# A two-block transformer kernel: five Q column blocks and half of the K splits become filler of the band attention, the bias table leaves by ScalarE's queue, and the rotary embedding runs on VectorE alone

## The chip, the cores and the metric

The kernel runs on one core of one Trainium2 chip. The core has TensorE (PE in the rows; PEld is its weight load), VectorE (DVE), ScalarE (ACT), GpSimd (POOL) and SyncE (SP), which here only issues DMAs. The metric is the device time of one execution in microseconds.

## The reference, cut to what matters

The program is two residual blocks, one after the other, on 512 tokens of width 1024. The change touches only the first block, which runs its layer twice (`DEPTH = 2`):

```
z = rms_norm(x, g) @ w_in[l]
q, k, v, cb, cc, cx, ga, gb = split(z)        # q 16 heads x 64, k and v 4 x 64, the rest 1024 each
q = partial_rope(q);  k = partial_rope(k)     # the first 16 of 64 dims are rotated
y_attn = band_attention(q, k, v, sink) @ w_attn_proj      # window of +-128 tokens
y_conv = (cb * short_conv(cc * cx, conv_w)) @ w_conv_proj # 3 taps along the tokens
mix = (sigmoid(ga) * y_attn + sigmoid(gb) * y_conv) @ w_out
x = x + rms_norm(mix);  x = x + rms_norm(ffn(rms_norm(x)))
```

The second block has four other attentions. Two of them add a bias that is looked up by distance in a small table (32 buckets by 8 heads). The kernel computes that table while the first block still runs, because the first block does not need it.

## The kernel before

Everything is feature-major: 128 features by 512 tokens are one block, and a matrix of 1024 features is eight blocks. The weights are packed on the host into units of 128x1024 float32 (512 KB), in the order in which they are used. A `Stream` loads a unit on SP's queue into one of three `raw` buffers (L255), ScalarE casts it to its high part `wh` (L267), and VectorE subtracts to get the low part `wl` (L268). One block of a product (`mblock`) is 24 matmuls: for each of 8 input blocks high x high, low x high and high x low (L513, L514, L515). A unit is cut two units ahead of its use, and a layer cuts 3 (layer 0) or 4 (layer 1) units beyond V ahead of time (`CA`).

After the norm, a layer does the following. The head computes K (two blocks, `pk`) and the first Q block; then V. VectorE forms the cosine and sine tables times the norm's factor (`ropeR`, L555). `rope` rotates a block: a multiplication of the PSUM block by the cosines (L563) and a shuffle of it (L564), both on VectorE, then a multiplication by the sines (L565) and a sum (L566), both on GpSimd. Each K head is split into `KH` (two casts on ScalarE, L577 and L578) and `KL` (two subtractions on VectorE, L579 and L580). Each Q block is split the same way (L595, L596). Before, all four K heads are split, V is evacuated (L586, L587), and all eight Q blocks are computed, rotated and split before the attention starts.

The band attention walks 16 heads in 18 steps: scores S, transposes of the softmax one step later, the product with V two steps later. Between these pieces it calls filler work from a list `bg`: before, the 24 blocks of the convolution branch (`conv_cc`, `conv_cx`, `conv_cb` for each of 8 columns). The order in which instructions stand on each engine is set by a scheduler of the framework, and each engine runs its list strictly in order.

The framework also gives each DMA one of eight completion semaphores in turn (DMAHW0 to DMAHW7). A DMA waits for the earlier DMA that used the same semaphore, whichever queue issued it.

After layer 0's attention, `bias_tables` makes the eight bias rows of 640 values with two small products, copies them to `row` (8 partitions), and writes each row 128 times to DRAM (`bias_d`, 2.62 MB) for the second block (L859). Then come eight blocks with the gate `gb` (L634) and eight with `w_conv_proj` (L639).

Of the kernel before, what the change touches and what calls it, by code (L numbers as in the profile page):

```python
# [9 lines left out]
F32 = mybir.dt.float32  # L10
F32R = mybir.dt.float32r
# [3 lines left out]
P = 128  # L15
T = 512
D = 1024
NB = 8
DEPTH = 2
NH = 16  # L20
# [8 lines left out]
U = 1024  # L29
# [35 lines left out]
def fm_units(w):  # L65
    m = w.shape[1] // P
    return w.reshape(NB, P, m, P).transpose(2, 1, 0, 3).reshape(m, P, U)


def tm_units(w, per):  # L70
    c = w.shape[1]
    u = w.reshape(NB // per, per, P, c).transpose(0, 2, 1, 3).reshape(NB // per, P, per * c)
    if per * c < U:
        u = np.concatenate([u, np.zeros((u.shape[0], P, U - per * c), u.dtype)], axis=2)
    return u


def down_units(w):
    t = w.reshape(NF, P, NB, P).transpose(2, 0, 1, 3).reshape(NF, 8, P, P)
    return t.transpose(0, 2, 1, 3).reshape(NF, P, U)  # L80


def pack(inp):
    units = []

    def put(u):
        units.append(u)

    for l in range(DEPTH):
        w = inp["w_in"][l]  # L90
        put(fm_units(w[:, 1024:1280]))
        put(fm_units(w[:, 0:128]))
        put(tm_units(w[:, 1280:1536], 4))
        put(fm_units(w[:, 128:1024]))
        cc, cx, cb = (fm_units(w[:, o:o + 1024]) for o in (2560, 3584, 1536))
        put(np.stack([cc, cx, cb], axis=1).reshape(24, P, U))
        put(fm_units(w[:, 5632:6656]))
        put(fm_units(inp["w_conv_proj"][l]))
        put(np.stack([fm_units(w[:, 4608:5632]), fm_units(inp["w_attn_proj"][l])], axis=1).reshape(16, P, U))
        put(fm_units(inp["w_out"][l]))  # L100
        put(np.stack([fm_units(inp["w_gate"][l]), fm_units(inp["w_up"][l])], axis=1).reshape(2 * NF, P, U))
        put(down_units(inp["w_down"][l]))
    w = inp["w_in_2"][0]
    o = np.cumsum([0, 256, 256, 256, 256, 256, 256, 4, 256, 256, 256, 256, 64, 64, 64, 64, 64, 64, 12])
# [7 lines left out]
    g = cat(dvs, dvw, bf, dg, dks, dkw)  # L112
    g = np.concatenate([g.reshape(NB, P, 272), np.zeros((1, P, 272), g.dtype)]).reshape(3, 3, P, 272)
    g = g.transpose(0, 2, 1, 3).reshape(3, P, 816)
# [70 lines left out]
    rope = np.stack([np.tile(ct, (2, 1)), np.tile(st, (2, 1))], axis=1).reshape(P, 2 * T)  # L185
# [94 lines left out]
class Kern:  # L280
# [249 lines left out]
    def layer(self, l, tail, pend):  # L530
        nc = self.nc
        h = Pair(self, "h", NB)
        acc2 = self.tmp("acc2")
        rs = {}
        head = Head(self, h, 3, seq=l == 0)
# [4 lines left out]
        pk = head.ps[0:2]  # L540
        wv = [self.st.next(ahead=1 + i) for i in range(2)]
        pv = [self.ps("pv") for _ in range(2)]
        for kb in range(NB):
            w = wv[kb // 4]
            sl = slice((kb % 4) * 256, (kb % 4) * 256 + 256)
            for tb in range(4):
                o = pv[tb // 2][:, (tb % 2) * 256:(tb % 2) * 256 + 256]
# [10 lines left out]
        C, S = cs[:, 0, :], cs[:, 1, :]  # L558
        perm = [(i + 8) % 16 if i < 16 else i for i in range(32)]

        def rope(ps):
            t1, t2 = self.tmp("t1"), self.tmp("t2")
            nc.vector.tensor_mul(t1, ps, C)  # L563
            nc.vector.stream_shuffle(t2, ps, perm)  # L564
            nc.gpsimd.tensor_mul(t2, t2, S)  # L565
            nc.gpsimd.tensor_add(t1, t1, t2)  # L566
            return t1

        KH, KL = FM(self, "KH", NKV, F32R), FM(self, "KL", NKV, F32R)
        lo_h, hi_h = slice(0, 64), slice(64, 128)  # L570
        for m in range(2):
            k = rope(pk[m])
            for j in range(2):
                src = k[64 * j:64 * j + 64]
                g = 2 * m + j
                own, oth = (lo_h, hi_h) if j == 0 else (hi_h, lo_h)
                nc.scalar.copy(KH[g][own], src)  # L577
                nc.scalar.copy(KH[g][oth], src)  # L578
                nc.vector.tensor_sub(KL[g][own], src, KH[g][own].bitcast(F32))  # L579
                nc.vector.tensor_sub(KL[g][oth], src, KH[g][own].bitcast(F32))  # L580
        V = FM(self, "V", 4, F32R)
        for tb in range(4):
            src = pv[tb // 2][:, (tb % 2) * 256:(tb % 2) * 256 + 256].rearrange("p (g d) -> p g d", g=4)
# [2 lines left out]
            nc.scalar.activation(vv[:, :, 0, :], src, AF.Copy, scale=r)  # L586
            nc.vector.scalar_tensor_tensor(vv[:, :, 1, :], src, r, vv[:, :, 0, :].bitcast(F32),  # L587
                                           op0=OP.mult, op1=OP.subtract)
        Q = FM(self, "Q", NH, F32R)
        for m in range(NB):  # L590
            q = rope(head.ps[2] if m == 0 else self.mblock(h))
            for j in range(2):
                hd = 2 * m + j
                own, oth = (lo_h, hi_h) if j == 0 else (hi_h, lo_h)
                nc.scalar.copy(Q[hd][own], q[own])  # L595
                nc.vector.tensor_sub(Q[hd][oth], q[own], Q[hd][own].bitcast(F32))  # L596

        y = FM(self, "y", NB, F32)
        cw = f"conv_w{l}"
# [20 lines left out]
            nc.vector.tensor_mul(t, self.mblock(h), self.R)  # L620
            nc.gpsimd.tensor_mul(y[m], t, cur.pop("c"))

        bg = [lambda m=m, f=f: f(m) for m in range(NB) for f in (conv_cc, conv_cx, conv_cb)]
        o = FM(self, "o", NB, F32)
        self.attend = True
        self.band_attention(l, Q, KH, KL, V, o, bg)
        self.attend = False
# [14 lines left out]
        for m in range(NB):  # L642
            g = self.tmp("ga")
# [100 lines left out]

    def band_attention(self, l, Q, KH, KL, V, o, bg):
        nc = self.nc
# [11 lines left out]
        def S(h):  # L758
# [4 lines left out]
            for i in range(4):  # L763
                n = HI[i] - LO[i]
                ps = self.ps("s")
                q = Q[h][:, i * P:(i + 1) * P]
                nc.tensor.matmul(ps[:, :n], q, KH[g][:, LO[i]:HI[i]], start=True, stop=False)  # L767
# [74 lines left out]
    def bias_tables(self):  # L842
        nc = self.nc
        oh = self.blk("oh", [33, 768], F32)
        nc.sync.dma_start(oh, self.a["onehot"])
        tab = self.small("tab", [33, 8], bufs=1)
        nc.sync.dma_start(tab, self.a["tab"])
        ohr = self.blk("ohr", [33, 768], F32R)
        nc.vector.tensor_copy(ohr, oh)
        tabr = [self.small(n, [33, 8], F32R, bufs=1) for n in ("tabh", "tabl")]  # L850
        self.split(*tabr, tab)
        row = self.blk("row", [8, 640], F32)
        for c0, c1, c2 in ((0, 512, 512), (512, 768, 640)):
            ps = self.ps("tb")
            for i, t in enumerate(tabr):
                nc.tensor.matmul(ps[0:8, :c1 - c0], t, ohr[:, c0:c1], start=i == 0, stop=i == 1)
            nc.scalar.copy(row[:, c0:c2], ps[0:8, :c2 - c0])
        self.bias_d = self.dramp.tile([8, P, 640], F32, name="bias_d")
        nc.sync.dma_start(self.bias_d, row[:, None, :].to_broadcast([8, P, 640]))  # L859

    def load_bias(self, h0):
        F = FM(self, "F", 4, F32)
# [530 lines left out]

    def sb_head(self, hd, Q, KH, KL, V, o):
        nc = self.nc
# [327 lines left out]
```

## Time and profile before

| | |
|---|---|
| time, median of 3 runs | 2560.83 us (2558.83 to 2562.65) |
| span of the profiled execution | 2559.2 us |
| TensorE busy | 2430.2 us, 95% of the span |
| VectorE busy | 1401.1 us, 55% |
| ScalarE busy | 1009.1 us, 39% |
| GpSimd busy | 500.3 us, 20% |
| mean granted TensorE clock | 0.973 of full speed |

The times are of whole executions; the span is that of the one execution that was profiled, from its first to its last instruction. TensorE is nearly always busy, so the table says where to look: at the few stretches in which TensorE is idle, or runs at a lower granted clock.

### The profile page before, as it was taken

The page shows a single profiled execution, that of the slowest core. Times are in us where ns is not written, and L with a number is a line of the kernel's source. Part 1 is how long each engine was busy: PE and PEld are TensorE (multiplying, and loading weights), DVE is VectorE, ACT ScalarE, POOL GpSimd, SP SyncE. Part 2 cuts the span into 40 slices and gives each one's busy share as a digit, 9 for nine tenths or more (in the row PEclk, how much of TensorE's full clock was granted, in tenths as well). Part 3 has the DMA queues.
Part 4 walks back from the last instruction along what each step waited for, and adds up shares of the span by engine and source line. Part 5 has one row for each costly group of instructions (what it writes and reads, how often), then busy time and mean ns, then how long its engine had stood idle before and what let it go on. Part 6 is the DMA issues. An engine that isn't in the chain of part 4 may idle for free.

```text
span 2559.2 us, 32881 instructions
## 1 busy us (share of the span) xinstructions
PE 2430.2 (95%) x12680; PEld 2090.4 (82%) x12680; DVE 1401.1 (55%) x2426; ACT 1009.1 (39%) x1885; POOL 500.3 (20%) x549
## 2 busy tenths in 40 slices
PE   8999779989999988999999899999698899999999
PEld 7888668888888887888888888888697888988888
DVE  7777343366643268776533676422667787644431
ACT  5455232343223243554323432222366576333320
POOL 4323000141110045321001411100411232100000
PEclk9999989989999999999999899999899899999999
DMA  4222442245423231213323354232320214222250
GB/s 140 85 73 71 86 121 91 82 141 196 180 102 124 91 128 42 75 66 103 107 82 99 124 214 180 92 98 91 106 88 26 82 44 132 80 93 93 95 179 29
DMA packets 84860, 264.37 MB, mean 103 GB/s; under 512 B 9023, under 2 KB 17855, under 8 KB 84704
## 3 DMA queue, kind: packets, MB, share of 16 engines
q1 hardware_dynamic: 84704, 262.27, 30.7%
q8 instruction: 100, 1.64, 0.3%
q14 instruction: 56, 0.46, 0.1%
HBM read 247.03 MB, written 15.20 MB: 102 GB/s over the span
## 4 chain that ended last, share of the span: by engine, by line
PE 87%; DVE 7%; ACT 2%; another core or an unknown queue 2%; issue 1%; POOL 0%; DMA 0%; SPq 0%; DVEq 0%; POOLq 0%; ACTq 0%
PE ps L513 24%; PE ps L515 24%; PE ps L514 23%; PE o L817 1%; PE pt L792 1%; PE tm L998 1%; PE tm L999 1%; PE tm L1000 1%; PE hd L514 1%; PE hd L513 1%; PE hd L515 1%; DVE wl L268 1%; PE s L768 1%; PE s L767 1%
## 5 line engine op out<-in xcount | busy, mean ns | idle before, releaser
L268 DVE TENSOR_TENSOR wl<-raw,wh 128x1024 fp32r<-128x1024 f32 x382 | 474.8, 1260 | 378.1 <-ACT wh L267 318.2
L267 ACT CAST wh<-raw 128x1024 fp32r<-128x1024 f32 x382 | 390.5, 1049 | 223.1 <-DMA raw<-in_w_dram 139.2
L513 PE MATMUL ps<-hh,wh 128*128 128x512 f32 x752 | 297.9, 396 | 37.1 <-ACT wh L267 37.1
L515 PE MATMUL ps<-hh,wl 128*128 128x512 f32 x752 | 298.2, 397 | 8.1 <-DVE wl L268 8.0
L514 PE MATMUL ps<-hl,wh 128*128 128x512 f32 x752 | 297.3, 395 | 0.0
L515 PE MATMUL ps<-hfh,wl 128*128 128x512 f32 x640 | 249.4, 390 | 1.5 <-DVE wl L268 1.5
L513 PE MATMUL ps<-hfh,wh 128*128 128x512 f32 x640 | 249.8, 391 | 0.0
L514 PE MATMUL ps<-hfl,wh 128*128 128x512 f32 x640 | 249.1, 389 | 0.0
L513 PEld LDWEIGHTS ps<-hh,wh 128*128 128x128 f32 x752 | 143.0, 190 | 65.6 <-ACT wh L267 38.3
L515 PEld LDWEIGHTS ps<-hh,wl 128*128 128x128 f32 x752 | 142.9, 190 | 37.2 <-DVE wl L268 9.9
L514 PEld LDWEIGHTS ps<-hl,wh 128*128 128x128 f32 x752 | 143.1, 190 | 27.5
L697 POOL TENSOR_TENSOR gs<-gs,R 128x512 f32<-128x512 f32 x44 | 70.9, 1612 | 390.6 <-ACT gs L376 390.6
L513 PE MATMUL ps<-hidh,wh 128*128 128x512 f32 (+1 forms) x396 | 145.2, 367 | 0.0
L515 PE MATMUL ps<-hidh,wl 128*128 128x512 f32 (+1 forms) x396 | 144.7, 365 | 0.0
L514 PE MATMUL ps<-hidl,wh 128*128 128x512 f32 (+1 forms) x396 | 144.7, 365 | 0.0
L376 ACT ACTIVATE pp<-pp,at_nm 128x256 f32<-128x256 f32 (+1 forms) x208 | 114.4, 553 | 71.2 <-DVE at_nm L774 60.3
L515 PEld LDWEIGHTS ps<-hfh,wl 128*128 128x128 f32 x640 | 120.2, 188 | 27.0 <-DVE wl L268 2.0
L513 PEld LDWEIGHTS ps<-hfh,wh 128*128 128x128 f32 x640 | 120.4, 188 | 24.7
L514 PEld LDWEIGHTS ps<-hfl,wh 128*128 128x128 f32 x640 | 120.2, 188 | 24.8
L514 PE MATMUL ps<-h3l,wh 128*128 128x512 f32 x320 | 124.5, 389 | 0.0
L515 PE MATMUL ps<-h3h,wl 128*128 128x512 f32 x320 | 124.5, 389 | 0.0
L513 PE MATMUL ps<-h3h,wh 128*128 128x512 f32 x320 | 124.3, 389 | 0.0
(460 smaller groups left out, 5427.8 us busy)
## 6 DMA issues: line engine op xcount, KB each, us to landing
raw<-in_w_dram SPq DMA_DIRECT2D x382, 512.0 KB, 3.5
adaraw<-in_ada_dram SPq DMA_DIRECT2D x48, 512.0 KB, 6.0
xd<-xh SPq DMA_DIRECT2D x24, 256.0 KB, 2.0
xh<-xd SPq DMA_DIRECT2D x24, 256.0 KB, 3.0
xh<-in_x_dram SPq DMA_DIRECT2D x16, 256.0 KB, 5.2
bias_d<-row SPq DMA_DIRECT2D x1, 2560.0 KB
xd<-fg SPq DMA_DIRECT2D x8, 256.0 KB, 2.9
F<-bias_d SPq DMA_DIRECT2D x8, 256.0 KB, 4.5
```

Of the source, the lines that this page charges most:

```text
L267: nc.scalar.copy(hi, raw)
L268: nc.vector.tensor_sub(lo, raw, hi.bitcast(F32))
L376: i = nc.scalar.activation(out, in_, func, **kw)
L513: nc.tensor.matmul(ps[:, t], w[0][:, sl], h.hi[kb][:, t], start=first, stop=False)
L514: nc.tensor.matmul(ps[:, t], w[0][:, sl], h.lo[kb][:, t], start=False, stop=False)
L515: nc.tensor.matmul(ps[:, t], w[1][:, sl], h.hi[kb][:, t], start=False, stop=last)
L697: nc.gpsimd.tensor_mul(g, g, self.R)
L767: nc.tensor.matmul(ps[:, :n], q, KH[g][:, LO[i]:HI[i]], start=True, stop=False)
L768: nc.tensor.matmul(ps[:, :n], q, KL[g][:, LO[i]:HI[i]], start=False, stop=True)
L792: nc.tensor.transpose(bank[:, c0:c0 + P], pslice(h, i)[:, c:c + P], self.ident)
L817: nc.tensor.matmul(ps[:, c0:c1], V[j][:, g * P:(g + 1) * P], t[b][:, a, c0:c1], start=(a == 0 and j == 0), stop=(a == 1 and j == 2))
L998: nc.tensor.matmul(o, h.hi[kb][:, tsl], w[0][:, sl], start=kb == 0 and i == 0, stop=False)
```

## The change

Four things change, all in the first block.

1. `rope` runs all four operations on VectorE.
2. K head 0 is split first, then the first Q block, then K head 1; K heads 2 and 3 are split from the filler list. The rotated second K block waits for that in a buffer of another pool (`xtile`).
3. Only Q blocks 0 to 2 are computed ahead of the attention. Blocks 3 to 7 join the convolution's 24 blocks in the filler list, one after each three. The first filler block is called before the attention, so 28 blocks and two K splits are left in the list. The weight units are packed in that order.
4. The bias table is written by eight DMAs of one row each, issued by ScalarE, in place of one DMA of eight rows, issued by SP.

```
+def mix_order():
+    seq = [(kind, m) for m in range(NB) for kind in range(3)]
+    for m in range(3, NB):
+        seq.insert(4 * (m - 3) + 3, ("q", m))
+    return seq
...
-        def rope(ps):
-            t1, t2 = self.tmp("t1"), self.tmp("t2")
+        def rope(ps, t1=None):
+            t1, t2 = t1 if t1 is not None else self.tmp("t1"), self.tmp("t2")
             nc.vector.tensor_mul(t1, ps, C)
             nc.vector.stream_shuffle(t2, ps, perm)
-            nc.gpsimd.tensor_mul(t2, t2, S)
-            nc.gpsimd.tensor_add(t1, t1, t2)
+            nc.vector.tensor_mul(t2, t2, S)
+            nc.vector.tensor_add(t1, t1, t2)
             return t1
...
-        for m in range(2):
-            k = rope(pk[m])
+        def k_split(k, g):
...
+        def q_block(m):
+            q_split(rope(self.mblock(h)), m)
+
+        k0 = rope(pk[0])
+        k_split(k0, 0)
+        q_split(rope(head.ps[2]), 0)
+        k1 = rope(pk[1], self.xtile("k1"))
+        q_block(1)
+        k_split(k0, 1)
         V = FM(self, "V", 4, F32R)
...
-        for m in range(NB):
-            q = rope(head.ps[2] if m == 0 else self.mblock(h))
...
+        q_block(2)
...
-        bg = [lambda m=m, f=f: f(m) for m in range(NB) for f in (conv_cc, conv_cx, conv_cb)]
+        conv = (conv_cc, conv_cx, conv_cb)
+        bg = [lambda f=q_block if kind == "q" else conv[kind], m=m: f(m) for kind, m in mix_order()]
+        bg.pop(0)()
+        bg.insert(2, lambda: k_split(k1, 2))
+        bg.insert(5, lambda: k_split(k1, 3))
...
-        nc.sync.dma_start(self.bias_d, row[:, None, :].to_broadcast([8, P, 640]))
+        for h in range(8):
+            nc.scalar.dma_start(self.bias_d[h:h + 1], row[h:h + 1, None, :].to_broadcast([1, P, 640]))
```

The first place is the start of layer 0's attention. On TensorE, after the third Q block (`ps_678`, last of the three whose units are cut ahead), stood a fourth Q block, with the first unit that is cut late (`wh_87`, `wl_88`):

```order
L515 MATMUL ps_678<-hh_21_154,wl_67_532 128x512
L513 MATMUL ps_720<-hh_10_120,wh_87_630 128x512
L514 MATMUL ps_720<-hl_11_121,wh_87_630 128x512
L515 MATMUL ps_720<-hh_10_120,wl_88_631 128x512
```

Now the third block is the first filler block (`ps_669`), and the first score matmuls stand ahead of the block with the late unit (`wh_85`, `wl_86`):

```order
L523 MATMUL ps_669<-hh_21_154,wl_67_532 128x512
L790 MATMUL s_698<-KH_72_547,Q_76_559 128x256
L791 MATMUL s_698<-KL_73_550,Q_76_559 128x256
L790 MATMUL s_702<-KH_72_547,Q_76_559 128x384
L791 MATMUL s_702<-KL_73_550,Q_76_559 128x384
L521 MATMUL ps_737<-hh_10_120,wh_85_620 128x512
L522 MATMUL ps_737<-hl_11_121,wh_85_620 128x512
L523 MATMUL ps_737<-hh_10_120,wl_86_621 128x512
```

On VectorE the part that ends with the late unit's `wl` reads, before, as follows; the four K heads' subtractions stand ahead of it:

```order
L587 SCALAR_TENSOR_TENSOR V_79_578<-pv_434,rs_r_321,V_79_578 128x4x64
L596 TENSOR_TENSOR Q_82_589<-t_80_583,Q_82_589 64x512 x2
L563 TENSOR_TENSOR t_90_661<-ps_636,ropeR_537 128x512
L564 STREAM_SHUFFLE t_91_662<-ps_636 128x512
L587 SCALAR_TENSOR_TENSOR V_78_573<-pv_433,rs_r_303,V_78_573 128x4x64
L587 SCALAR_TENSOR_TENSOR V_79_578<-pv_434,rs_r_321,V_79_578 128x4x64
L596 TENSOR_TENSOR Q_86_625<-t_84_619,Q_86_625 64x512 x2
L268 TENSOR_TENSOR wl_88_631<-raw_351,wh_87_630 128x1024
```

Now it reads as follows, and ahead of it, from `ropeR` on, stand in all five multiplications by the cosines, five shuffles, five multiplications by the sines, four sums, four K and four Q subtractions and two of V:

```order
L573 TENSOR_TENSOR t_81_596<-t_81_596,ropeR_537 128x512
L596 TENSOR_TENSOR Q_76_559<-t_74_553,Q_76_559 64x512 x2
L574 TENSOR_TENSOR t_80_595<-t_80_595,t_81_596 128x512
L571 TENSOR_TENSOR t_88_651<-ps_626,ropeR_537 128x512
L572 STREAM_SHUFFLE t_89_652<-ps_626 128x512
L596 TENSOR_TENSOR Q_82_601<-t_80_595,Q_82_601 64x512 x2
L573 TENSOR_TENSOR t_89_652<-t_89_652,ropeR_537 128x512
L613 SCALAR_TENSOR_TENSOR V_83_610<-pv_433,rs_r_303,V_83_610 128x4x64
L613 SCALAR_TENSOR_TENSOR V_84_615<-pv_434,rs_r_321,V_84_615 128x4x64
L276 TENSOR_TENSOR wl_86_621<-raw_351,wh_85_620 128x1024
```

The K heads 1 to 3 have gone from eight subtractions ahead of the late unit to two of head 1, and the sines and sums have come in from GpSimd. Layer 1 reads alike, with four units cut ahead and five sums and six Q subtractions ahead of its late unit.

The second place is ScalarE's list at the end of layer 0's attention, with the semaphores that each instruction waits for. Now the eight table DMAs stand ahead of the casts of the units raw39 (`raw_2748`) and raw40 (`raw_2785`):

```order
L880 COPY row_2836<-tb_2841 8x128 [waits PE_49]
L883 DMA bias_d<-row_2836 128x1x640 [waits Activation_49]
L883 DMA bias_d<-row_2836 128x1x640 [waits DMAHW5_49]
L883 DMA bias_d<-row_2836 128x1x640 [waits DMAHW7_49]
L883 DMA bias_d<-row_2836 128x1x640
L883 DMA bias_d<-row_2836 128x1x640 [waits DMAHW1_49]
L883 DMA bias_d<-row_2836 128x1x640 [waits DMAHW2_49]
L883 DMA bias_d<-row_2836 128x1x640 [waits DMAHW3_49]
L883 DMA bias_d<-row_2836 128x1x640 [waits DMAHW4_49]
L513 CAST yph_551_2887<-y_126_835 128x512 x2
L384 ACTIVATE z_547_2854<-z_547_2854 128x512 [waits DVE_49]
L275 CAST wh_553_2891<-raw_2748 128x1024
```

The first of the eight raises semaphore DMAHW4, so the eighth waits until the first has landed. The others raise DMAHW5, 7, 0, 1, 2 and 3.

The third place is SP's list at the same point. Before, the table's one DMA stood between raw40 and raw41:

```order
L255 DMA raw40_2785<-in_w_dram 128x1024 [waits DMAHW5_49,DMAHW3_49,DVE_49]
L859 DMA bias_d_2845<-row_544_2836 1024x1x640 [waits DMAHW4_49,Activation_49]
L255 DMA raw41_2852<-in_w_dram 128x1024 [waits DMAHW7_49,DVE_49]
```

Now it is gone, and the loads that follow wait, by the semaphores, for the table's rows: raw42 for the second (DMAHW5), raw44 for the third (DMAHW7), raw45 to raw48 for the fourth to the seventh (DMAHW0 to DMAHW3), and raw49 for the eighth (DMAHW4):

```order
L263 DMA raw41_2859<-in_w_dram 128x1024 [waits DMAHW0_49,DVE_49]
L263 DMA raw42_2895<-in_w_dram 128x1024 [waits DMAHW5_49,DMAHW2_49,DVE_49]
L263 DMA raw43_2930<-in_w_dram 128x1024 [waits DMAHW6_49,DMAHW3_49,DVE_49]
L263 DMA raw44_2966<-in_w_dram 128x1024 [waits DMAHW7_49,DVE_49]
L263 DMA raw45_3001<-in_w_dram 128x1024 [waits DMAHW5_49,DMAHW0_49,DVE_49]
L263 DMA raw46_3037<-in_w_dram 128x1024 [waits DMAHW6_49,DMAHW1_49,DVE_49]
L263 DMA raw47_3072<-in_w_dram 128x1024 [waits DMAHW7_49,DMAHW2_49,DVE_49]
L263 DMA raw48_3108<-in_w_dram 128x1024 [waits DMAHW3_49,DMAHW0_49,DVE_49]
L263 DMA raw49_3144<-in_w_dram 128x1024 [waits DMAHW4_49,DMAHW1_49,DVE_49]
```

What moved on SP is one issue out of its list, and eight waits for another queue's transfers into it. Apart from these three places the lists of the later parts are nearly unchanged, and TensorE has as many matmuls as before.

## Rows read from the trace of the kernel before

**Rows 1.** The page: busy us, share and instructions by engine.

```profile
PE 2430.2 (95%) x12680; PEld 2090.4 (82%) x12680; DVE 1401.1 (55%) x2426; ACT 1009.1 (39%) x1885; POOL 500.3 (20%) x549
```

**Rows 2.** TensorE's own waits, whole span: total us, times, longest.

```profile
PE ps L513 <- ACT wh L267: 37.1, 3, 31.3
```

**Rows 3.** TensorE's timeline at four places: start, duration, instruction, [idle before, releaser].

```profile
60.13 0.50 PE L513 MATMUL ps<-hh,wh 128*128 128x512 f32 x1 [1.25 <-ACT wh L267]
...
65.17 0.80 PE L515 MATMUL ps<-hh,wl 128*128 128x512 f32 x1 [4.31 <-DVE wl L268]
...
990.59 0.79 PE L513 MATMUL ps<-hh,wh 128*128 128x512 f32 x1 [4.48 <-ACT wh L267]
...
995.52 0.80 PE L515 MATMUL ps<-hh,wl 128*128 128x512 f32 x1 [3.71 <-DVE wl L268]
...
336.09 0.80 PE L513 MATMUL ps<-hh,wh 128*128 128x512 f32 x1 [31.33 <-ACT wh L267]
```

**Rows 4.** Windows: engines' busy us (instructions), granted clock, DMA share, GB/s.

```profile
65.20:71.10 5.90, 5.90 (x14) 4.70 (x15) 5.77 (x7) 1.61 (x3) 3.31 (x2) 0.50 0.28 92
...
100.00:280.00 180.00, 180.00 (x958) 155.47 (x958) 131.65 (x299) 102.73 (x247) 50.81 (x72) 1.00 0.23 79
986.10:999.50 13.40, 5.21 (x12) 3.64 (x12) 13.08 (x15) 5.71 (x8) 9.15 (x6) 0.62 0.11 39
...
580.00:600.00 20.00, 18.47 (x82) 14.93 (x81) 13.35 (x18) 8.82 (x13) 5.68 (x4) 1.00 0.40 147
```

**Rows 5.** ScalarE's timeline, start of layer 0's attention.

```profile
45.96 0.63 ACT L577 CAST KH<-t 64x512 fp32r<-64x512 f32 x1 [6.61 <-POOL t L566]
```

**Rows 6.** VectorE's timeline there.

```profile
39.39 1.23 DVE L555 TENSOR_TENSOR ropeR<-rope,R 128x1024 f32<-128x1024 f32 x1 [3.73 <-ACT R L502]
40.65 0.69 DVE L563 TENSOR_TENSOR t<-hd,ropeR 128x512 f32<-128x512 f32 x1
...
41.26 0.75 DVE L564 STREAM_SHUFFLE t<-hd 128x512 f32<-128x512 f32 x1
...
47.74 1.69 DVE L580 TENSOR_TENSOR KL<-t,KH 64x512 fp32r<-64x512 f32 x1
...
51.15 0.69 DVE L580 TENSOR_TENSOR KL<-t,KH 64x512 fp32r<-64x512 f32 x1
...
56.48 0.88 DVE L587 SCALAR_TENSOR_TENSOR V<-pv,rs_r,V 128x256 fp32r<-128x256 f32 x2
...
63.89 1.22 DVE L268 TENSOR_TENSOR wl<-raw,wh 128x1024 fp32r<-128x1024 f32 x1
```

**Rows 7.** VectorE's timeline, start of layer 1's attention.

```profile
964.75 1.23 DVE L555 TENSOR_TENSOR ropeR<-rope,R 128x1024 f32<-128x1024 f32 x1 [3.73 <-ACT R L502]
```

**Rows 8.** ScalarE's timeline after the table's write, and VectorE's.

```profile
335.00 1.04 ACT L267 CAST wh<-raw 128x1024 fp32r<-128x1024 f32 x1 [44.12 <-DMA raw<-in_w_dram]
...
388.74 0.68 DVE L639 TENSOR_TENSOR z<-ps,z 128x512 f32<-128x512 f32 x1
```

**Rows 9.** SP's timeline from 278 us, and the source view of L255, 280 to 281 us.

```profile
278.93 0.82 SPq L859 DMA_DIRECT2D bias_d<-row  x1
...
280.04 19.28 SPq L255 DMA_DIRECT2D raw<-in_w_dram  x1
...
DMA to landing us min/median/max: 54.9/54.9/54.9
```

**Rows 10.** Windows during the write, at its end, and one with loads only (columns as in rows 4).

```profile
288.00:292.00 4.00, 4.00 (x19) 3.30 (x19) 0.69 (x1) 1.66 (x3) 0.00 (x0) 1.00 0.47 49
...
336.10:340.80 4.70, 4.66 (x10) 3.27 (x11) 3.85 (x5) 2.81 (x5) 0.00 (x0) 0.51 0.58 179
...
820.00:840.00 20.00, 20.00 (x90) 16.58 (x89) 3.68 (x3) 3.89 (x5) 1.29 (x1) 1.00 0.35 122
```

**Rows 11.** The page's DMA issues: KB each, median us from issue to landing.

```profile
raw<-in_w_dram SPq DMA_DIRECT2D x382, 512.0 KB, 3.5
...
xd<-xh SPq DMA_DIRECT2D x24, 256.0 KB, 2.0
```

More of the change, by code (lines that the diff above doesn't have):

```diff
@@ L93, in pack @@
         put(tm_units(w[:, 1280:1536], 4))
-        put(fm_units(w[:, 128:1024]))
-        cc, cx, cb = (fm_units(w[:, o:o + 1024]) for o in (2560, 3584, 1536))
-        put(np.stack([cc, cx, cb], axis=1).reshape(24, P, U))
+        q = fm_units(w[:, 0:1024])
+        conv = [fm_units(w[:, o:o + 1024]) for o in (2560, 3584, 1536)]
+        put(q[1:3])
+        put(np.stack([q[m] if kind == "q" else conv[kind][m] for kind, m in mix_order()]))
         put(fm_units(w[:, 5632:6656]))
@@ L570, in layer, with q_split @@
         lo_h, hi_h = slice(0, 64), slice(64, 128)
-        for m in range(2):
-            k = rope(pk[m])
+        def k_split(k, g):
+            j = g % 2
+            src = k[64 * j:64 * j + 64]
+            own, oth = (lo_h, hi_h) if j == 0 else (hi_h, lo_h)
+            nc.scalar.copy(KH[g][own], src)
+            nc.scalar.copy(KH[g][oth], src)
+            nc.vector.tensor_sub(KL[g][own], src, KH[g][own].bitcast(F32))
+            nc.vector.tensor_sub(KL[g][oth], src, KH[g][own].bitcast(F32))
+        Q = FM(self, "Q", NH, F32R)
+        def q_split(q, m):
             for j in range(2):
-                src = k[64 * j:64 * j + 64]
-                g = 2 * m + j
+                hd = 2 * m + j
                 own, oth = (lo_h, hi_h) if j == 0 else (hi_h, lo_h)
[L577 to L580, printed above, removed]
+                nc.scalar.copy(Q[hd][own], q[own])
+                nc.vector.tensor_sub(Q[hd][oth], q[own], Q[hd][own].bitcast(F32))
+        def q_block(m):
[6 more added lines that the diff above has]
+        k_split(k0, 1)
         V = FM(self, "V", 4, F32R)
@@ L588, in layer @@
                                            op0=OP.mult, op1=OP.subtract)
-        Q = FM(self, "Q", NH, F32R)
-        for m in range(NB):
-            q = rope(head.ps[2] if m == 0 else self.mblock(h))
[L592 to L596, printed above, removed]
+        q_block(2)
         y = FM(self, "y", NB, F32)
```

## The prediction

> **What bounds the kernel now.** I read four views in this order. The page first: TensorE is busy for 95% of the span [rows 1], so a change pays only where TensorE waits or runs at half its clock; what it takes off other engines pays nothing by itself. Then TensorE's waits: the largest entry is 37.1 us in three waits for a `wh`, one of them of 31.3 us [rows 2]. Then the timeline at these places: five waits for a late weight unit, 1.25 and 4.31 us at the start of layer 0's attention, 4.48 and 3.71 us at that of layer 1's, 31.33 us behind the bias table's write [rows 3]. Last the windows. [...] In the attention itself (100 to 280 us) TensorE is busy all the time and VectorE for 131.65 of 180 us, 73% [rows 4].
>
> So there are three sums to win: 8.5 us at layer 0's start, 10.8 at layer 1's, 33.7 at the table. All else is bound by TensorE's matmuls, whose number doesn't change.
>
> **The two attention starts.** The late unit is late because ScalarE and VectorE first split four K heads. ScalarE waits 6.61 us for GpSimd's last rotation step before its first K cast [rows 5], and VectorE's K subtractions take up to 1.69 us beside GpSimd's work, 0.69 alone [rows 6]. After the change VectorE does in a row, from the end of `ropeR` at 40.6 us to the first late `wl`: ten steps of the cosine and shuffle kind at 0.65 (from starts 40.65 and 41.26 [rows 6]), 6.5 us; five sine steps, four sums, four K and four Q subtractions at 0.69, 11.7 us; two V steps, 0.9, and the `wl` itself, 1.2. That is 20.3 us, so the `wl` is there at about 61. TensorE's three blocks that are cut ahead end at 58.9 (60.13 less 1.25 [rows 3]); two pairs of scores (1280 columns, where a block's matmul of 512 takes 0.22) take 0.6, two matmuls that need only `wh` 0.4. TensorE then waits some 1.3 us instead of 5.6. The cover of the moved work is these scores; if the 20.3 us were 3 longer, the old wait would be back. A wait of that size needs no lower clock: in 580 to 600 us TensorE lost 1.5 us at clock 1.00 [rows 4]. I take 1.4 left of 8.5: **-7.1**.
>
> Layer 1 likewise: `ropeR` ends at 966.0 [rows 7]; ahead of its late `wl` stand one sum, two Q subtractions and two convolution evacuations more, 20.3 + 5 x 0.69 = 23.8, so 989.8. TensorE's four blocks end at 986.1 (990.59 less 4.48 [rows 3]), three pairs of scores take 0.9 us and two matmuls 0.4, and the wait left is about 2.4: **-8.4**.
>
> **Inside the attention.** Each moved Q block brings TensorE 24 matmuls (90 in 20 us [rows 10], so 5.3 us), and VectorE 0.65 x 2 for cosine and shuffle, 0.69 x 4 for sine, sum and Q split, 1.2 for `wl`: 5.3 us too. Five blocks and the split of two K heads (2.8 us) add 29 us to VectorE and 27 to TensorE. Over the attention VectorE goes from 73% to (131.65 + 29) / (180 + 27) = 78%. That leaves slack on the average, but TensorE's waits come from queues that are late, not from averages: in the first 30 us the four K and V leftovers, the rotations and the first score evacuations stand behind each other. I bound this by 0 and 8 us for both layers and take **+3**. GpSimd's two rotation steps per block were off TensorE's path inside the attention, so their removal is worth nothing there.
>
> **The bias table.** Before, one DMA read eight rows and landed so that the next load, issued at 280.04, came in 54.9 us later [rows 9], where a load takes 3.5 [rows 11]; so the write took 51 us. ScalarE waited 44.12 us for that load [rows 8]. During the write the DMA engines were busy at 0.47, half of them, and moved 49 GB/s, 6.5 for a busy engine; with loads alone it is 122 GB/s at 0.35, 21.8 for a busy engine [rows 10]. So the engines are not the limit; a store of 256 KB to DRAM lands in 2.0 us [rows 11], so DRAM is hardly it; what is left is the source, eight rows on eight partitions.
>
> The change puts the rows on another queue, but it reads them one after the other, and the loads wait for them all the same: raw49 may be issued only when the eighth row has landed. If that takes W us from the first row's issue, raw49's block ends W + 3.5 (landing) + 1.04 (cast) + 1.22 (`wl`) + 5.3 (matmuls) = W + 11 after it. Before, that block was evacuated at 388.74 [rows 8], 108.7 after 280.04. The stage loses W - 97.6 us against before, and wins at most the 33.7 above. W decides, then, and no row shows it. Below: if each engine keeps its 6.5 GB/s and all sixteen work, the 2.62 MB take 26 us and the whole 33.7 are won. Above: if a row alone can't be read faster than a busy engine works in the loads, 21.8 GB/s, W is 120 us and 22 are lost. The row nearest is the write itself: its eight sources gave 49 GB/s together, and one can't give more than all. If they share one way out, one row gets the 49 and W stays 53; if two, 24.5, and W is near 103. I take W = 103, because a load's engine, which works on one partition row at a time, reaches 21.8 and not 49: 5.4 lost.
>
> [...]
>
> Two smaller costs lie in the same stage. The eighth DMA waits on ScalarE for the first row's landing, an eighth of W, 13 us, and behind it stand the casts of raw39 and raw40. TensorE has 25 us of cut units at that point (280 to 304.8, where its 31.33 us began [rows 3]), so this costs about 4 us that the later wait swallows. And the loads share the DMA engines with the rows: if they take turns, a load comes in no faster than a row, each load is issued only when a row lands, and the last loads bunch behind the eighth row; that costs between 0 and one row's time less one block's, 13 - 5 = 8 us. I take 3.6 of it, and in all **+9** for the stage. [...]
>
> **The sum.** -7.1 - 8.4 + 3 + 9 = -3.5. The profiled span is 2559.2 us; the median of the runs is 1.6 above it. 2559.2 - 3.5 + 1.6 = 2557 us.
>
> **The rivals.**
> First, the table is hidden: the rows come out fast enough (W under 64, where no load is late). Then the stage wins 33.7 and the sum is -7.1 - 8.4 + 3 - 33.7 = -46.2, so 2515 us. For it: only half the DMA engines were busy [rows 10], and a DMA of 128 repeats of one row may use all. Against it: a busy engine moved a third of its usual rate. 14%.
> Second, slower: VectorE becomes the bound of the attention's first half. There each group of four filler blocks costs TensorE 21 us and VectorE 12.4 (5.3 for Q; 7.1 for a convolution column, five steps of 0.69 and three `wl`). The 2.4 heads that go with it cost VectorE (131.65 - 8 x 7.1) / 16 = 4.7 us each, another 11, and bring TensorE to 29. VectorE has 5 us of slack in 29; it decides against the change when waits for GpSimd and ScalarE on VectorE's queue eat more than that. At 1 us for each of 36 steps: +36 in place of the 3, sum +29.5, so 2590; at half of it 2572. Against it: TensorE was busy throughout from 100 to 280 us [rows 4]. 11%.
> The forecast itself, starts won and the table's wait spread out rather than gone, has the remaining 75%.
>
> **How the numbers follow.** 2557 is the forecast's case; its own range is 2545 to 2574, from W = 97 without sharing and without new waits to W = 110 with all of both. What a measurement of this kernel can tell from no change is 0.2%, 5.1 us. Within the forecast's case faster by more than that needs a table term under 7.4 us: 0.45 of it; slower needs one over 17.6: 0.10; the rest is the same. With the first rival all faster and the second nearly all slower: faster 0.14 + 0.34 = 0.48, same 0.34, slower 0.18. The range is that of the forecast's case, widened below to starts won whole (-19.3) and W of 92, above by W of 114: 2536 to 2578. It leaves out the first rival and half of the second.
>
> **What would show it.** The 31.33 us wait should be gone as one wait, and come back as several of some 7 us, each for a `wh` whose load waited on SP for one of ScalarE's DMAs. SP should show those waits, ScalarE one of about 12 us at the eighth DMA. The DMA windows should show about 25 GB/s besides the loads' over some 100 us. At the two attention starts TensorE's waits should sum to 3 to 4 us at full clock. GpSimd should have 40 instructions fewer, VectorE 40 more and some 28 us (40 x 0.69). If the table's stage shows no waits, W is wrong; if TensorE waits for `ptb` or PSUM inside the attention, the second rival holds.

## The result and the profile after

The changed kernel takes 2590.5 us (median of 4 runs, 2590.0 to 2591.0), the one before 2560.1 in the same session: a ratio of 1.0116, 95% interval 1.0102 to 1.0131. Slower, where 2557 was forecast. The number is that of the second rival, but not its mechanism, as the stages below show.

TensorE's waits in the profile of the changed kernel (which wait; us in all, times, longest) answer to [rows 2]:

```profile
PE ps L521 <- ACT wh L275: 69.4, 7, 57.6
```

The waits on which the argument rests, in order of time (start, us of the instruction, in brackets the idle time before it and its releaser), answer to [rows 3]:

```profile
60.76 0.50 PE L523 MATMUL ps<-hh,wl 128*128 128x512 f32 x1 [0.41 <-DVE wl L276]
89.06 1.44 PE L840 MATMUL o<-ptb,V 128*128 128x256 f32 x8 [0.97 <-DVE at_m L793]
105.41 0.44 PE L790 MATMUL s<-KH,Q 128*128 128x384 f32 x1 [0.70 <-DVE ptb L514]
347.31 0.80 PE L521 MATMUL ps<-hh,wh 128*128 128x512 f32 x1 [57.60 <-ACT wh L275]
372.84 0.79 PE L521 MATMUL ps<-hh,wh 128*128 128x512 f32 x1 [7.14 <-ACT wh L275]
1021.02 0.79 PE L521 MATMUL ps<-hh,wh 128*128 128x512 f32 x1 [3.48 <-ACT wh L275]
1022.73 0.79 PE L523 MATMUL ps<-hh,wl 128*128 128x512 f32 x1 [0.50 <-DVE wl L276]
```

Layer 0's two waits are all but gone (0.41 of 5.56), layer 1's are halved, and the one behind the table has grown from 31.33 to 57.60 with a second of 7.14. The windows of layer 0's start, of the long wait and of layer 1's start (columns as in [rows 4]) show full clock at the first and half clock at the two others, and hardly any work of VectorE or ScalarE during the long wait:

```profile
59.00:65.00 6.00, 5.59 (x27) 4.38 (x26) 5.91 (x10) 4.48 (x7) 0.00 (x0) 1.00 0.28 90
292.60:347.30 54.70, 0.00 (x0) 0.00 (x0) 1.31 (x3) 2.65 (x5) 0.00 (x0) 0.50 0.93 36
1019.60:1026.50 6.90, 4.99 (x11) 3.49 (x12) 6.81 (x14) 4.58 (x7) 0.00 (x0) 0.51 0.25 76
```

Why nothing works there stands in ScalarE's timeline (ACTq is its issuing of DMAs; the first rows are the first two issues, then three, then the last three, in windows that overlap):

```profile
274.76 1.22 ACTq L883 DMA_DIRECT2D bias_d<-row  x2
276.02 33.19 ACTq L883 DMA_DIRECT2D bias_d<-row  x3
309.25 35.36 ACTq L883 DMA_DIRECT2D bias_d<-row  x3
344.65 0.62 ACT L513 CAST yph<-y 128x512 fp32r<-128x512 f32 x1 [69.92 <-DMA bias_d<-row]
```

Two one-row DMAs are issued in 0.6 us each. From the third on an issue takes 9 to 12 us, and ScalarE does nothing else until 344.6: no cast of a weight for 70 us. The table's DMAs (issue to landing in the last column) and the loads beside them, 275 to 380 us, and SP's waits from 260 to 380:

```profile
raw<-in_w_dram SPq DMA_DIRECT2D x6, 512.0 KB, 22.7
bias_d<-row ACTq DMA_DIRECT2D x8, 320.0 KB, 37.8
```

```profile
SPq L263 <- DVE wl L276: 73.3, 5, 47.1
SPq L263 <- DMA bias_d<-row: 25.1, 1, 25.1
```

A load takes 22.7 us (the median of six) instead of the 3.5 of [rows 11]. The table's packets run from 276.0 to 370.5: W, the time that the eight rows take, is 94.5 us, at 27.7 GB/s.

The two waits behind the table have different ends. SP issued one load during the hold, at 275.86 us (raw41). The source view of that one issue says when it landed:

```profile
DMA to landing us min/median/max: 25.7/25.7/25.7
```

So it lay there from 301.5 on, behind two units that were issued before the hold, and nothing was cast until ScalarE was free. The next load (raw42) waited on SP first for the second row, 25.1 us, and then for a buffer, 47.1 us, since nothing was cast; it was issued at 348.54. The wait of 57.60 us thus ends with ScalarE's hold, and the one of 7.14 us with raw42's slow load.

I cut each kernel's span at five instructions of TensorE: the first matmul of the table (`tb`), the last of `w_conv_proj`'s blocks (`yph`, `ypl`), layer 1's last V matmul, its last `o` matmul, and the end. Each column is how much longer a stage took than before, in us, from one profiled execution each; the runs are told below.

| kernel | median us | to the table | table stage | to layer 1's V | its attention | rest |
|---|---|---|---|---|---|---|
| changed kernel | 2590.5 | -4.2 | +35.7 | -1.5 | +1.3 | -1.2 |
| p1_sp_table | 2553.5 | -4.7 | -0.2 | -3.5 | +1.0 | -1.4 |
| p2_act_alone | 2599.7 | -0.8 | +35.1 | +0.7 | +0.4 | +2.4 |
| p3_act_one | 2538.1 | -4.4 | -15.1 | -3.0 | +1.1 | -1.5 |
| p4_pool_rows | 2578.4 | -4.6 | +23.7 | -1.6 | +1.3 | -1.0 |
| p13_two_act | 2577.6 | -4.3 | +24.5 | -3.5 | +1.1 | -1.4 |
| p16_64_rows | 2596.3 | -4.5 | +49.8 | -2.3 | -6.1 | -2.6 |
| p12_rows_spread | 2559.0 | -4.3 | +4.8 | -2.4 | +1.9 | -1.4 |
| p6_spread_act | 2520.1 | -4.9 | -34.0 | -1.9 | +1.1 | -1.3 |
| p7_spread_sp | 2520.5 | -4.8 | -34.0 | -3.0 | +1.1 | -1.4 |
| p15_spread_alone | 2527.2 | 0.0 | -34.0 | -0.2 | -0.1 | +0.1 |
| p9_rope_alone | 2558.5 | +1.1 | -0.2 | -2.5 | -0.9 | +1.6 |
| p8_pb_pin | 2550.2 | -4.1 | -0.3 | +0.2 | -6.7 | -1.0 |
| p10_q_alone | 2548.3 | -3.5 | +0.6 | -1.6 | -6.9 | -1.3 |
| p11_best | 2516.3 | -4.5 | -34.0 | -0.1 | -6.7 | -1.1 |
| p14_q_spread | 2515.5 | -3.4 | -34.0 | -1.9 | -6.8 | +2.2 |

The loss is one stage's, the table's; and layer 1's attention, from which 7 us were expected, gave nothing. The columns "to layer 1's V" and "rest", to which the change adds no work, differ by up to 3.5 us from the kernel before, and that is left unexplained.

### The profile page after: what moved, and what is told of

It is laid out like the page before. It is cut to its first block, busy times and chain, and to the rows that moved or that the text cites. A ratio compares the mean times of both kernels' runs of the same rounds, so it can differ in the third digit from the quotient of the medians.

```text
span 2589.3 us, 32823 instructions
## 1 busy us (share of the span) xinstructions
PE 2431.9 (94%) x12680; PEld 2089.8 (81%) x12680; DVE 1405.5 (54%) x2466; ACT 1008.2 (39%) x1885; POOL 439.3 (17%) x509
## 3 DMA queue, kind: packets, MB, share of 16 engines
q10 hardware_dynamic: 1152, 2.62, 3.3%
## 4 chain that ended last, share of the span: by engine, by line
PE 84%; DVE 8%; ACT 3%; ACTq 3%; DMA 1%; issue 1%; POOL 0%; SPq 0%; DVEq 0%; POOLq 0%
PE ps L521 23%; PE ps L523 23%; PE ps L522 23%; ACTq L883 3%; PE o L840 1%; PE tm L1022 1%; PE tm L1023 1%; PE tm L1024 1%; PE hd L522 1%; DMA raw<-in_w_dram 1%; PE hd L523 1%; PE hd L521 1%; PE pt L815 1%; DVE wl L276 1%; DVE xh L499 1%
## 6 DMA issues: line engine op xcount, KB each, us to landing
bias_d<-row ACTq DMA_DIRECT2D x8, 320.0 KB, 37.8
```

## Experiments on the table

Theory A: ScalarE, held in issuing, casts nothing. Theory B: the one-row DMAs are slow, and the loads beside them crawl whatever ScalarE does. Theory C is the second rival, VectorE in the attention.

**p1_sp_table and p2_act_alone.** The table's line of either kernel in the other.

```
-        for h in range(8):
-            nc.scalar.dma_start(self.bias_d[h:h + 1], row[h:h + 1, None, :].to_broadcast([1, P, 640]))
+        nc.sync.dma_start(self.bias_d, row[:, None, :].to_broadcast([8, P, 640]))
```

> The changed kernel, with the bias table written as before by one DMA of eight rows on SP's queue; Q, K and rotation edits stay. Theory A (ScalarE is held while it issues the eight one-row DMAs, so that no weight is cast) and theory B (the one-row DMAs are slow, and the weight loads beside them crawl, whatever ScalarE does) both put the whole loss into the table: the wait behind the table comes back at some 31 us, layer 0's attention ends 4.2 us earlier than before, layer 1's part costs 1.3 us more, and the time is 2560 - 4.2 + 1.3 = 2557 us, 2552 to 2560. Theory C (VectorE bound by the rotations and Q columns in the attention) keeps most of the loss: 2580 us or more.

> The kernel before, with nothing changed but the bias table: eight one-row DMAs on ScalarE's queue. A and B: the wait of 31.3 us becomes one of some 58 and a second one of some 7, layer 0's stage loses 31 to 36 us, and the time is 2591 to 2596 us. C: no loss, 2560 us.

2553.5 us (ratio 0.9970, 0.9958 to 0.9982) and 2599.7 (1.0148, 1.0134 to 1.0162). The table alone makes the loss, +35 us with either attention; without it the change gains 7.5. C falls. p2_act_alone lies 3.7 us above its range: its table stage is within what was expected, and the rest of the excess, in the other columns, is left unexplained.

**p4_pool_rows and p13_two_act.** All eight rows (p4), or the last six (p13, below), from GpSimd's queue.

```
-            nc.scalar.dma_start(self.bias_d[h:h + 1], row[h:h + 1, None, :].to_broadcast([1, P, 640]))
+            eng = nc.scalar if h < 2 else nc.gpsimd
+            eng.dma_start(self.bias_d[h:h + 1], row[h:h + 1, None, :].to_broadcast([1, P, 640]))
```

> The changed kernel, with its eight one-row DMAs issued on GpSimd's queue; neither ScalarE nor SP issues a row. A: the rows still take some 94 us, but ScalarE casts what SP loads; the waits behind the table fall from 64.7 us to 31 or less, and the time is 2557 us or less. B: the rows hold the loads, and ScalarE has nothing to cast; the waits stay at 50 to 65 us, and the time is 2575 to 2590 us.

> The changed kernel, with the first two of its eight one-row DMAs on ScalarE's queue (their issues took 0.6 us each) and the other six on GpSimd's. Theory A in the size that the run with all eight on GpSimd gave it (12 us of the loss come from the issues from the third on, which hold ScalarE): as that run, 2575 to 2582 us. If ScalarE's queue slows the loads in another way than by holding ScalarE, or is held by two rows already, 2585 to 2591.

2578.4 and 2577.6 us: 12 to 13 less than the changed kernel. With ScalarE free, the wait of p4_pool_rows falls into three, each for a load that came late; below them ScalarE's own waits for loads (270 to 400 us), and the loads and rows from 275 to 380 us:

```profile
332.29 0.79 PE L521 MATMUL ps<-hh,wh 128*128 128x512 f32 x1 [26.72 <-ACT wh L275]
353.57 0.80 PE L521 MATMUL ps<-hh,wh 128*128 128x512 f32 x1 [12.64 <-ACT wh L275]
371.89 0.80 PE L521 MATMUL ps<-yph,wh 128*128 128x512 f32 x1 [10.06 <-ACT wh L275]
```

```profile
ACT wh L275 <- DMA raw<-in_w_dram: 80.9, 8, 39.4
```

```profile
raw<-in_w_dram SPq DMA_DIRECT2D x9, 512.0 KB, 38.3
bias_d<-row POOLq DMA_DIRECT2D x8, 320.0 KB, 54.7
```

The three waits sum to 49.4 us, which is neither A's 31 nor B's 50. So both theories hold a share, and the two overlap. Freeing ScalarE wins 12 of the stage's 35.7 us (A, and only from the third issue on, since two rows on ScalarE cost nothing). With ScalarE free the stage still loses 24 us against the narrow eight-row write, to loads that take 38 us beside the rows (B). In the changed kernel itself the hold hides most of B, as its long wait showed. What B would cost there without the hold is not shown exactly: GpSimd's queue moves the rows in 640 packets and ScalarE's in 1152, and the loads beside them took 38.3 and 22.7 us.

**p3_act_one.** The eight rows in one DMA, on ScalarE's queue.

> The changed kernel, with the table written by one DMA of eight rows on ScalarE's queue. The rows come out of eight partitions at once, as before, in some 52 us, and ScalarE has one issue (0.8 us) and no second one behind it. A: ScalarE is free, the loads run on SP's queue beside the table, and the wait is at most the 31 us of before: 2530 to 2557 us. B, in the form that loads crawl beside any such write: the wait stays near 31 us and the time near 2557; if the loads crawl more than that, 2565 and above.

2538.1 us (0.9908, 0.9894 to 0.9921). One issue of 1.26 us holds nobody, W is 54.6, and a load beside it takes 19.4 us, which kept TensorE fed until 316.7. One wait of 15.36 us is left, and it isn't for a load: the late unit was issued at 297.60 us and landed 19.4 later, at 317.0, but ScalarE's cast of it waited on until the table's write had landed:

```profile
330.94 1.04 ACT L275 CAST wh<-raw 128x1024 fp32r<-128x1024 f32 x1 [25.62 <-DMA bias_d<-row]
```

The likely reason stands in the source: `row` and `wh` are drawn from one pool of buffers (`blk`), so the cast must wait for the write to have read a buffer that it reuses. No run shows it by another buffer for `row`. In the stage's column, moving the write off SP's queue won 15 us, and cutting it into rows lost 51 (from -15.1 to +35.7).

**p6_spread_act, p7_spread_sp and p15_spread_alone.** The same packets, from partitions four apart (p6 on ScalarE's queue, p7 on SP's, p15 on the kernel before; the matmul and the copies write 32 rows instead of 8):

```
+        tabz = self.small("tabz", [33, 32], bufs=1)
+        nc.vector.memset(tabz, 0.0)
+        nc.vector.tensor_copy(tabz[:, 0:32:4], tab)
-        row = self.blk("row", [8, 640], F32)
+        row = self.blk("row", [32, 640], F32)
-        nc.sync.dma_start(self.bias_d, row[:, None, :].to_broadcast([8, P, 640]))
+        nc.sync.dma_start(self.bias_d, row[0:32:4, None, :].to_broadcast([8, P, 640]))
```

> The changed kernel, with the eight rows on partitions 0, 4, 8, ... 28 instead of 0 to 7, written by one DMA on ScalarE's queue. Same bytes, same packets as in the run with one DMA on ScalarE's queue (2538 us, W = 54.5 us, a wait of 15.4 us), only the source's partitions lie further apart. Theory P (the way out of neighbouring partitions is the limit: 2.62 MB in 52 us from eight neighbours, 94.5 us from one partition at a time): the rows come out at the 21.8 GB/s that an engine reaches in the loads, eight engines in some 15 to 20 us, no wait is left behind the table, and the time is 2518 to 2524 us. Theory E (an engine repeats a row at 6.6 GB/s wherever it lies): W stays over 50 us and the time 2535 to 2541.

> The same eight spread partitions, one DMA, but on SP's queue ahead of the loads, as the kernel before has it. P: the loads behind it in the queue come 15 to 20 us after it, TensorE's cut units cover that, and the time is 2520 to 2527 us; then it doesn't matter whose queue it is. E: as the changed kernel with one DMA on SP's queue, 2550 to 2556 us, with a wait of 31 us.

> The kernel before, with only the eight spread partitions in its one DMA on SP's queue. Theory P: the 31.3 us wait and its 2.3 us at half clock go, 2561 - 33.5 = 2528 us, 2525 to 2531; the difference of this run to the run with the spread table and all the other edits (2520.5) is then what Q, K and rotation are worth, 7.5 us. If the loads that come earlier change the waits further on, more than 3 us beside that.

2520.1 (0.9836), 2520.5 (0.9838) and 2527.2 us (0.9869, 0.9855 to 0.9883). No wait is left behind the table, and 34.0 us are won on every base. The stretch behind the first issue reads so in three kernels (columns as in [rows 4], the last two the DMA engines' busy share and GB/s): first p7_spread_sp, then p1_sp_table in the middle of its wait, then the changed kernel.

```profile
276.00:280.00 4.00, 4.00 (x19) 3.30 (x19) 1.71 (x3) 1.13 (x3) 0.00 (x0) 1.00 0.51 206
```

```profile
316.00:326.00 10.00, 0.00 (x0) 0.00 (x0) 0.00 (x0) 0.00 (x0) 0.00 (x0) 0.50 0.47 49
```

```profile
306.00:316.00 10.00, 0.00 (x0) 0.00 (x0) 0.00 (x0) 0.00 (x0) 0.00 (x0) 0.50 0.90 27
```

The same bytes go at 206 GB/s from eight partitions four apart, at 49 from eight neighbours and at 27 from one at a time; the whole write takes 13.4 us in p7_spread_sp, 17.4 in p6_spread_act and 53.0 in p1_sp_table. Neither the queue nor the DMA engines made the write slow, but where its source lies.

**p12_rows_spread.** The changed kernel's eight DMAs, rows four partitions apart.

> The changed kernel's eight one-row DMAs on ScalarE's queue, but with the rows on partitions 0, 4, ... 28 instead of 0 to 7. Theory P-row (a row read by itself comes out by one way, and the rows of one queue go in order): nothing changes, W stays 93 to 96 us, ScalarE is held as before, 2587 to 2593 us. Rival (two rows are under way at a time, so neighbours got into each other's way in the changed kernel): W falls to about half, some 48 us, and the time to 2540 to 2560 us.

2559.0 us; my theory fell, and the time lies in the rival's range. W is 60.1, though each DMA still reads one partition: rows under way together had been in each other's way as neighbours. ScalarE is still held:

```profile
ACT yph L513 <- DMA bias_d<-row: 48.6, 1, 48.6
```

**p16_64_rows.** Each row in eight DMAs of 16 copies.

> The changed kernel, with each of its eight one-row DMAs on ScalarE's queue cut into eight of 16 copies, 64 in all; same bytes from the same partitions, 2560 bytes a packet. Theory N (an issue waits when more than two DMAs are under way): the third is held already, each later one for an eighth of a row's time, 1.4 us, ScalarE is held some 90 us, 2600 to 2612 us. Theory M (it waits when the packets of some two rows are still to be moved): the first 16 to 20 issues take 0.6 us each, the later ones 1.4, the hold ends with W less two rows' time, as before, and the time is 2586 to 2596 us.

2596.3 us. The first five issues take 0.6 us each, nearly all later ones 1.4 to 1.6 (the thirteenth 2.1, the fourteenth 0.8); just behind the thirty-third, the first of row 4, one of 1.1 and four of 0.6 stand in between. ScalarE's timeline at the first five, at 27 of the long ones and there:

```profile
274.44 3.12 ACTq L884 DMA_DIRECT2D bias_d<-row  x5
278.90 43.08 ACTq L884 DMA_DIRECT2D bias_d<-row  x27
322.02 3.65 ACTq L884 DMA_DIRECT2D bias_d<-row  x5
```

Neither theory has it: five is more than two DMAs, and less than the packets of two rows. What an issue waits for stays open; that it follows the rows' pace doesn't (1.4 to 1.6 us an issue, where the changed kernel's W over 64 is 1.5).

## Experiments on the attention

**p9_rope_alone and p10_q_alone.** The rotation alone on the kernel before (below), and on p1_sp_table the same lines put back:

```
-            nc.gpsimd.tensor_mul(t2, t2, S)
-            nc.gpsimd.tensor_add(t1, t1, t2)
+            nc.vector.tensor_mul(t2, t2, S)
+            nc.vector.tensor_add(t1, t1, t2)
```

> The kernel before, with only the rotation's last two steps moved from GpSimd to VectorE. Theory Q (the attention starts gain by the K and Q splits that move behind them): no gain, 2559 to 2566 us, since VectorE has four more steps of 0.69 us in the start for each block that GpSimd no longer does. Rival R (ScalarE's wait of 6.6 us for GpSimd's sum was the cause): the starts win 5 us or more each, 2548 to 2554 us.

> The changed kernel with the table as before by one DMA on SP's queue (2553.5 us), and the rotation's last two steps back on GpSimd; the Q blocks and K splits stay in the filler work. In this build the spreading matmuls of layer 1 stand ahead of the last V matmul again. If VectorE's rotation is what let the starts win, both starts' waits come back in part: 2557 to 2563 us. If moving K and Q alone wins them, and the order of the matmuls in layer 1 with them, 2547 to 2553 us.

2558.5 us (0.9991, 0.9982 to 1.0000) and 2548.3 (0.9946, 0.9933 to 0.9958). The rotation on VectorE gains nothing measurable by itself; the gain is the moved Q and K work's. p10_q_alone takes 5 us less than p1_sp_table, but that is not the rotation's price: its build also has another order of matmuls in layer 1, and its gain stands in layer 1's attention (-6.9 for +1.0). p8_pb_pin below has that order with the rotation on VectorE and gains as much there; between the two lie 1.9 us, within their intervals.

**p8_pb_pin.** Why layer 1 gained nothing stands in TensorE's program order. Before, the matmul `pb`, from which `R` and then `ropeR` come, has four V matmuls still behind it:

```
L550 MATMUL pv_7560<-wl_1159_7468,hh_1112_7237 128x256
L425 MATMUL pb_7458<-dg_7456,ones 128x256
L551 MATMUL pv_7560<-wh_1158_7467,hl_1113_7238 128x256
```

Now it stands behind the last V matmul, with twelve of the Q blocks' in between (the expectation below miscounts both):

```
L559 MATMUL pv_7567<-wh_1158_7474,hl_1113_7245 128x256
...
L521 MATMUL ps_7709<-hh_1106_7224,wh_1160_7480 128x512
L433 MATMUL pb_7465<-dg_7463,ones 128x256
L522 MATMUL ps_7709<-hl_1107_7225,wh_1160_7480 128x512
```

The run holds it, and the `pc` matmuls that it waits for, ahead of V's last ones:

```
+                if l == 1 and (kb, tb) == (3, 0):
+                    for m in self.pcs:
+                        self.order(mm, m)
+                if l == 1 and (kb, tb) == (7, 2):
+                    self.order(mm, self.last_pb)
```

> The changed kernel with the table as before by one DMA on SP's queue (2553.5 us), and in layer 1 alone TensorE's matmuls that spread 1/RMS (pc and pb, on which R and the rotary table wait) held ahead of the last V matmuls, where the kernel before has them; in the changed kernel pb stands 11 rows behind the last V matmul, in the one before 6 rows ahead. Theory S (layer 1's start gained nothing because these matmuls came later): the rotary table is there 4 us earlier, the waits of 3.5 and 1.0 us and the half clock behind them go, and the time is 2547 to 2550 us. Rival (ScalarE's Q casts, which stand ahead of the weight's cast, set the start): less than 1.5 us change, 2552 to 2555.

2550.2 us (0.9955, 0.9942 to 0.9967). In its windows the stretch to layer 1's last V matmul and the attention behind it read:

```profile
929.60:960.30 30.70, 24.34 (x183) 23.52 (x182) 20.29 (x31) 10.58 (x25) 14.04 (x15) 0.89 0.42 143
960.30:1189.50 229.20, 226.37 (x1161) 193.49 (x1160) 179.97 (x388) 121.81 (x274) 52.38 (x72) 1.00 0.23 75
```

The attention takes 229.2 us at full clock throughout, against 236.8 in p1_sp_table: 7.6 won, of which the V stretch, 26.9 there, takes back 3.8. The timed gain of 3.3 us is at the edge of what the intervals tell (they overlap), but three runs say the same unasked: in p10_q_alone, p14_q_spread and p16_64_rows `pb` again has four V matmuls behind it, and there too layer 1's attention is 6 to 7 us shorter, while it is 1.0 to 1.9 us longer in the seven runs (p1, p3, p4, p6, p7, p12, p13) where `pb` stands as in the changed kernel. The cleanest of the three is p16_64_rows, whose source differs from the changed kernel's in the table's DMAs alone. Layer 1's attention in the changed kernel, then in p16_64_rows:

```profile
994.50:1231.60 237.10, 230.20 (x1162) 195.08 (x1161) 181.56 (x388) 122.95 (x275) 50.52 (x72) 0.99 0.22 73
```

```profile
1007.80:1237.30 229.50, 226.67 (x1158) 193.22 (x1158) 180.91 (x388) 121.87 (x274) 54.25 (x73) 1.00 0.23 75
```

**p11_best and p14_q_spread.** The spread table with the pinned order, and with the rotation back on GpSimd.

> The two remedies together: eight spread partitions in one DMA on SP's queue (2520.5 us) and layer 1's spreading matmuls held ahead of the last V matmuls (3.3 us of gain beside the narrow table). If the two places don't touch each other, 2516 to 2518.5 us; if the loads that come earlier after the spread table take away what the order wins, 2519 to 2521.

> Spread partitions in one DMA on SP's queue, the Q blocks and K splits in the filler work as in the changed kernel, the rotation's last two steps back on GpSimd. If the 5 us that GpSimd's rotation won beside the narrow table and the 33 us of the spread table add, 2548.3 - 33 = 2515 us, 2513 to 2518; if the order of the instructions in layer 1 turns again in this build, 2520 to 2524.

2516.3 us (0.9823, 0.9809 to 0.9836) and 2515.5 (0.9820, 0.9806 to 0.9834): equal, and 1.8% below the kernel before. The gains add. Of the two, p11_best has the rotation on VectorE and p14_q_spread on GpSimd, so here too its place is worth nothing measurable.

## Why the prediction was wrong

**The table stage: +9 forecast, +35.7 measured.** W was not the fault: 94.5 us, where I took 103. No run shows the W of 97 at the lower end of the forecast's own range; the changed kernel showed 94.5 in its place. The step that failed is the one from W to the loss. By the prediction's own W - 97.6 the measured W gives a gain of 3.1, so the two "smaller costs" had to bring 38.8 us, where I took 3.6:

- "The eighth DMA waits on ScalarE for the first row's landing, 13 us": I priced the semaphore that the program names, and not the issuing itself. ScalarE was held from the third DMA on, for 69 us: an issue took 9 to 12 us, about as long as a row (94.5 / 8 = 11.8). The row was in front of me: SP's load behind the table took 19.28 us to issue [rows 9], and I read only its landing. Freeing ScalarE won 12 us in p4 and p13.
- "that costs between 0 and one row's time less one block's, 8 us": loads were to come one for each row. They took 23 us (38 with ScalarE free), and TensorE used one in 5.3 (24 matmuls, at 90 in 20 us [rows 10]). With ScalarE free that cost 24 us in p4 and p13. The forecast of several waits of 7 us, each for an SP wait, was wrong with it; SP shows one such wait.

The path was wrong with them. I had the stage end with raw49 behind the eighth row. The last wait in it is raw42's, seven units earlier: the hold kept it from being issued until 348.54, the rows kept it from landing for another 23.2 us, and from 372.84 on TensorE had 57 us of blocks left and no wait.

**Layer 0's start: right.** -7.1 forecast; of 5.56 us idle 0.41 is left and no half clock, -8.1. Each of the three sums to win holds, beside its waits of [rows 3], what TensorE lost behind them at the lower clock: 2.95 us here (busy for 5.9 us at 0.50) and 2.6 at layer 1's start (13.4 us at 0.62, half speed for 10.2 of them, TensorE busy for 5.2) by [rows 4], 2.3 behind the table (busy for 4.66 us at 0.51) by [rows 10].

**Layer 1's start: -8.4 forecast; its whole attention came out 1.3 us longer.** The start's waits were halved, 8.19 us before and 3.98 now, and other waits came up inside the attention. The 23.8 us of VectorE's work were about right: in p1_sp_table `ropeR` ends at 961.2 and the late matmul starts at 984.27. What failed is "`ropeR` ends at 966.0", 1.5 us behind the last V matmul (964.50), carried over as if it stayed: it ends 5.1 behind it there (956.05), since `pb` moved. With `pb` held in place (p8_pb_pin) this attention gained 6.7, where -8.4 and half of the +3 made -6.9. The last V matmul before, then the last V matmul, `ropeR` and the late matmul in p1_sp_table:

```profile
964.50 0.28 PE L551 MATMUL pv<-wh,hl 128*128 128x256 f32 x1
```

```profile
956.05 0.28 PE L559 MATMUL pv<-wh,hl 128*128 128x256 f32 x1
959.97 1.23 DVE L563 TENSOR_TENSOR ropeR<-rope,R 128x1024 f32<-128x1024 f32 x1 [5.05 <-ACT R L510]
984.27 0.80 PE L523 MATMUL ps<-hh,wl 128*128 128x512 f32 x1 [1.00 <-DVE wl L276]
```

**Inside the attention: +3 for both layers was too little.** Layer 0's stage won 4.2 where its start won 8.1, so 3.9 went there: waits of 0.97 and 0.70 and smaller ones, and 160 transposes that stood 0.107 us apart on the mean instead of 0.094, 2.2 us.

**The second rival** has the right number by chance: p1_sp_table keeps all its VectorE work and takes 2553.5. The sign that I had named for it did come, a wait for `ptb` of 0.70 us, and was too weak a sign. **The first**, a hidden table at 2515 us, is the time that p11 and p14 reach, by another write than the change's.

**VectorE's time.** It has the forecast 40 instructions more (2466), but 1405.5 us instead of 1401.1 + 28:

```profile
PE 2431.9 (94%) x12680; PEld 2089.8 (81%) x12680; DVE 1405.5 (54%) x2466; ACT 1008.2 (39%) x1885; POOL 439.3 (17%) x509
```

Without the rotation on GpSimd its other steps got shorter. The K subtraction, 0.69 to 1.69 us before [rows 6], in the changed kernel, in p9_rope_alone and, with the rotation back on GpSimd, in p10_q_alone (ns: least, median, most):

```profile
L587 DVE TENSOR_TENSOR KL<-t,KH x4: 684/686/689, 50.4 to 1011.0; 64x512 fp32r<-64x512 f32 x4
```

```profile
L580 DVE TENSOR_TENSOR KL<-t,KH x8: 684/686/689, 47.6 to 977.5; 64x512 fp32r<-64x512 f32 x8
```

```profile
L587 DVE TENSOR_TENSOR KL<-t,KH x4: 687/1188/1687, 47.9 to 972.1; 64x512 fp32r<-64x512 f32 x4
```

## What to carry to other kernels

Before a DMA is cut up or moved to another engine, look where its source lies: eight rows four partitions apart made a write of 53 us one of 13, and no queue did. Price an issue by the rows that show one behind a long transfer, for a compute engine that issues can be held nearly as long as its DMAs last (here 70 us of 94.5). And when code that feeds a critical chain is moved, look in the new program order at that chain's own instructions, the small matmuls too, before carrying a time over from the old trace.

The table isn't read until late (its first load is issued at 1941.4 us), so a slow write in small pieces was another way; it wasn't tried:

```profile
L889 SPq DMA_DIRECT2D F<-bias_d x8: 326/422/437, 1941.4 to 2096.0; - x8
```

## What was not expected of the hardware

In p16_64_rows four issues in a row went quickly again, in 0.6 us each, at one place alone, where the rows pass from partition 3 to 4. Why there, no run shows. And one-row DMAs of one queue are under way together: in p12_rows_spread one takes 22.2 us from issue to landing (the median), and all eight take 60.1; as neighbours they took 37.8 and 94.5.
